# Score tiles by parity and half: 416 keys instead of 512 in the dilated attention of a hybrid block

## The chip, the cores and the metric

The kernel runs on one core of one Trainium2 chip. The metric is the device time of one execution in microseconds (us): the median of three runs for the kernel before and, later, for the changed one. A profile is of one further execution, with its own time and with the span from its first to its last instruction.

## What is computed

One encoder layer over 512 tokens of width 2048. Two mixers read the same projection; the change touches the first, attention with 16 heads of 64. Three dilated patterns share one softmax, so a query sees a key if any pattern allows the distance:

```python
for window, dilation in ((128, 1), (512, 4), (2048, 16)):
    o_p, lse_p = dilated_window_attention(aq, ak, av, rel_bias, window, dilation)
    # keys at 0, +-dilation, ... +-window/2
mix_w = jax.nn.softmax(jnp.stack(lses, axis=0), axis=0)
att = jnp.einsum('pbsh,pbshe->bshe', mix_w, jnp.stack(outs, axis=0))
```

Odd distances are allowed by the first pattern alone, up to 64; the others have even distances only. The rest of the layer (adaLN, the gated linear attention GLA, gates, output projection, norms) stays as it is.

## The kernel before

TensorE's matmuls take fp32 data as a rounded high part and a low part: `three` (lines 221 to 223) adds high x high, high x low and low x high. The kernel goes through the layer in stages: conditioning and the first products (tiles `sta`, `stb`), then units of projection products (`qk2`, `qk4`, `qk6`, `gk`, then values, gates, output). A unit has 8 groups of weights, 64 ticks of three 512-column products each, and a list of side work with places between 0 and 1 that `unit` puts between the ticks. The order of TensorE is this written order; DVE, ACT, POOL and SP get theirs from the tile framework. SP's queue issues nearly all loads and the copies from SBUF to SBUF, in order.

The attention is side work of the four units `qk2` to `gk`, four heads each. A head has four score tiles of 128 queries by 512 keys:

- `qk_evict` (lines 736 to 748) takes queries (reversed) and keys of two heads from PSUM. `qs` holds the high part in one half of the partitions and the low part in the other; `ks` and `kl` hold the keys' high and low part in both halves, the second copy by DMA.
- `score` multiplies `qs` with `ks` and with `kl` (lines 787, 788), adds the bias from `g` and finds the row's extreme on DVE (791), exponentiates on ACT (794), scales on POOL (801). `g` is a table of biases shifted by a column per partition, so that a slice of it fits a tile of reversed queries; it is loaded from `grow` in DRAM.
- `turn`, two tiles later, transposes four blocks of 128 x 128 (line 813) and writes high and low parts of the turned block `pt` (817 on ACT, 818 on DVE). `pt` covers two tiles, 256 queries; the pool has room for two such blocks.
- `values`, three tiles after the second of its two score tiles, multiplies `pt` with the values `vv` (line 827, eight matmuls) and adds up into `cat` (830, 834).

The items' places come from `ATT_AT`: start 0.17, span 0.8, and shifts of the first two and the last. Weights come through four `raw` buffers; `fetch` asks for them two groups ahead. Small sums for other stages (`S`, `rawv`) run on DVE beside the scores.

Of the kernel before, what the change touches and what calls it, by code (L numbers as in the profile page):

```python
# [79 lines left out]
def _runs():  # L80
# [6 lines left out]
    for j in range(2):  # L87
        cols = np.arange(512 * j, min(512 * j + 512, NREL))
        part = []
        for b, v in enumerate(seen):  # L90
            c = cols[bucket[cols] == v] - 512 * j
            if len(c):
                assert len(c) == c[-1] + 1 - c[0]
                if len(c) == 1 and part and part[-1][3]:
# [15 lines left out]
ATT_AT = (0.17, 0.8, 0.04, 0.05, 0.05)  # L110
# [72 lines left out]
def block_kernel(ctx: ExitStack, tc: tile.TileContext, a: dict):  # L183
# [6 lines left out]
    t2 = mid.enter_context(tc.tile_pool(name="t2", bufs=16))  # L190
# [144 lines left out]
    def row_part(j, i):  # L335
# [4 lines left out]
        for lo, hi, b, single in RUNS[j][i]:  # L340
            if single:
                tt(t[:, lo:hi], t[:, lo:hi], rel[:, b:b + hi - lo], op=ALU.subtract)
# [192 lines left out]
    def sum_col():  # L535
        psb["col"] = PJ("psc")
        for i in range(4):
            mm(psb["col"][:, i:i + 1], ssum[:, i * P:i * P + P], ones[:, 0:1], start=True, stop=True)
# [25 lines left out]
    def first_products(z, e):  # L564
# [3 lines left out]
        for i in range(4):  # L568
            j, t = 4 * z + i, slice(P * i, P * i + P)
# [4 lines left out]
    def products(st, k, j):  # L574
# [3 lines left out]
        if st == "a":  # L578
            t, c = slice(j % 4 * P, j % 4 * P + P), slice(j // 4 * 512, j // 4 * 512 + 512)
# [85 lines left out]
    for z in range(4):  # L665
        task(("row", z), "ACT", 0.9, [("uh", 7 + z), "rowl"], 50, lambda z=z: row_part(z // 2, z % 2))
# [60 lines left out]

    def qk_evict(p, psq, psk):
# [3 lines left out]
        for j in range(2):  # L732
            own = slice(64 * j, 64 * j + 64)
            oth = slice(64 - 64 * j, 128 - 64 * j)
            qs = T2(f"qs{p}{j}", F32R)
            act(qs[own], psq[own, ::-1], AF.Copy, scale=-0.125)
            stt(qs[oth], psq[own, ::-1], -0.125, qs[own].bitcast(F32),
                op0=ALU.mult, op1=ALU.subtract)
            stacks[2 * p + j] = [qs, None, None, own]
        for j in range(2):  # L740
            own = slice(64 * j, 64 * j + 64)
            oth = slice(64 - 64 * j, 128 - 64 * j)
            ks = T2(f"ks{p}{j}", F32R)
            kl = T2(f"kl{p}{j}", F32R)
            act(ks[own], psk[own], AF.Copy)
            nc.sync.dma_start(ks[oth].bitcast(F32), ks[own].bitcast(F32))
            tt(kl[own], psk[own], ks[own].bitcast(F32), op=ALU.subtract)
            nc.sync.dma_start(kl[oth].bitcast(F32), kl[own].bitcast(F32))
            stacks[2 * p + j][1:3] = ks, kl
# [16 lines left out]

    def attention(pairs):

        tiles = [(2 * p + j, i) for p in pairs for j in range(2) for i in range(4)]
        gt, pt, pr_ = {}, {}, {}  # L770
        heads = [2 * p + j for p in pairs for j in range(2)]

        def g_load(h):
            g = gp.tile([P, 896], F32, tag="g", name=f"g{h}")
            nc.sync.dma_start(g, bass.AP(grow.tensor, grow.offset + h * 1024, [[1, P], [1, 896]]))
            gt[h] = g

        def score(h, i):
            def go():
# [4 lines left out]
                qs, ks, kl, _ = stacks[h]  # L784
                q = slice(P * i, P * i + P)
# [920 lines left out]
```

## Time and profile before

| what | value |
|---|---|
| median of three runs | 919.68 us (919.38 to 919.89) |
| time of the profiled execution | 919.28 us |
| its span | 917.5 us |
| granted TensorE clock, mean | 0.996 of full |
| the attention's part of the span | about 190 to 455 us |
| one unit of it (qk4, from its first transposition to that of qk6) | 66.3 us |
| score tiles, turned tiles, value groups | 64, 64, 32 |
| bytes moved by DMA | 238.13 MB, 260 GB/s in the mean |

A line of the costliest groups has the source line, the engine, the operation, output and input tiles with shapes and the count, then busy us and mean ns of one, then the engine's idle time before them and what ended it. Matmuls are pipelined: the busy time of one overlaps the next, and what one costs is read from the distance of the starts.

### The profile page before, as it was taken

To read this page: it belongs to the slowest core of one execution; us is meant where nothing else is said; L and a number is where in the kernel's file an instruction comes from. 1 tells how busy PE (TensorE), PEld (TensorE's weight loads), DVE (VectorE), ACT (ScalarE), POOL (GpSimd) and SP (SyncE) were. 2 spreads that over 40 slices of the span, in tenths; PEclk is the share of its full clock that TensorE was granted. 3 is DMA by queue.
4 is the path that set the end of the run, shared out by engine and by line. 5 is a ranking of instruction groups with operands and counts; after the bars stand their busy time and mean duration, and the time that the engine had idled before them with its cause. 6 is when DMAs were issued, how large, how long until landed. Compare 5 with 4: busy or idle time off the path is not lost.

```text
span 917.5 us, 12263 instructions
## 1 busy us (share of the span) xinstructions
PE 902.5 (98%) x4327; PEld 749.9 (82%) x4327; DVE 715.8 (78%) x1043; ACT 490.7 (53%) x790; POOL 113.4 (12%) x168
## 2 busy tenths in 40 slices
PE   8999999999999999999999999999999999999996
PEld 6888888888888888888878788888888888888884
DVE  8988799877778878877659668586686649798786
ACT  5553533565555655655657554363654238455464
POOL 0000000012323223222100101111120100000001
PEclk9999999999999999999999999999999999999998
DMA  9999498567789898886778869877787887877863
GB/s 350 406 413 398 165 358 321 185 190 208 215 233 282 246 251 252 246 238 207 218 241 261 283 212 278 261 206 237 213 289 212 265 276 264 291 294 241 303 224 149
DMA packets 61671, 238.13 MB, mean 260 GB/s; under 512 B 8133, under 2 KB 8421, under 8 KB 52265
## 3 DMA queue, kind: packets, MB, share of 16 engines
q1 hardware_dynamic: 54850, 195.03, 59.6%
q0 software_dynamic: 6464, 42.01, 20.0%
q8 instruction: 34, 0.56, 0.2%
q10 hardware_dynamic: 296, 0.30, 0.1%
q14 instruction: 27, 0.22, 0.1%
HBM read 224.64 MB, written 50.42 MB: 300 GB/s over the span
## 4 chain that ended last, share of the span: by engine, by line
PE 90%; DVE 4%; DMA 2%; ACT 2%; issue 1%; SPq 0%; DVEq 0%; ACTq 0%
PE ps_qk L221 5%; PE ps_qk L222 5%; PE ps_qk L223 5%; PE g L223 4%; PE g L222 4%; PE g L221 4%; PE o L827 3%; PE stb L223 3%; PE stb L222 3%; PE stb L221 3%; PE t L813 3%; PE ps_ag L221 3%; PE ps_ag L223 3%; PE ps_ag L222 3%; PE sta L222 3%; PE sta L223 3%
## 5 line engine op out<-in xcount | busy, mean ns | idle before, releaser
L794 ACT ACTIVATE p<-p,st 128x512 f32<-128x512 f32 x64 | 46.2, 723 | 55.0 <-DVE st L791 54.6
L320 DVE CUSTOM_DVE_ANT_0 cb<-cb,sb,c_bcond 128x2048 f32<-128x2048 f32 (+1 forms) x32 | 73.5, 2297 | 0.3 <-DMA cb<-in_wm 0.2
L801 POOL TENSOR_SCALAR p<-p,st 128x512 f32<-128x512 f32 x62 | 47.7, 770 | 185.1 <-DVE st L797 135.8
L791 DVE CUSTOM_DVE_ANT_0 p<-s,g 128x512 f32<-128x512 f32 x64 | 43.8, 686 | 16.4 <-PE s L788 14.1
L818 DVE TENSOR_TENSOR pt<-t,pt 128x512 fp32r<-128x512 f32 x64 | 43.8, 688 | 12.0 <-ACT pt L817 11.5
L817 ACT ACTIVATE pt<-t 128x512 fp32r<-128x512 f32 x64 | 37.9, 592 | 11.7 <-PE t L813 10.9
L421 POOL DMA_DIRECT2D T<-in_w_o x32 | 23.2, 724 | 165.7 <-ACT V2h L485 13.7
L813 PEld LDWEIGHTS t<-c_ident,p 128*128 128x128 f32 x256 | 31.4, 140 | 9.7 <-POOL p L801 1.3
L813 PE MATMUL t<-c_ident,p 128*128 128x128 f32 x256 | 38.5, 273 | 0.1
L827 PEld LDWEIGHTS o<-pt,vv 128*128 128x128 f32 x256 | 34.7, 188 | 2.9
L827 PE MATMUL o<-pt,vv 128*128 128x256 f32 x256 | 35.5, 281 | 0.0
L787 PE MATMUL s<-ks,qs 128*128 128x512 f32 x64 | 25.1, 392 | 0.0
L788 PE MATMUL s<-kl,qs 128*128 128x512 f32 x64 | 25.0, 390 | 0.0
L1000 ACT ACTIVATE sq<-st,sc 128x256 f32<-128x256 f32 x24 | 12.2, 508 | 19.3 <-DVE st L990 11.3
L320 DVE CUSTOM_DVE_ANT_0 rawg<-rawg,crow,c_bcond 128x1024 f32<-128x1024 f32 x16 | 20.3, 1280 | 2.0 <-DMA rawg<-in_wg 2.0
L320 DVE CUSTOM_DVE_ANT_0 rawg<-rawg,crow,gate 128x1024 f32<-128x1024 f32 x16 | 20.4, 1280 | 0.8 <-DMA rawg<-in_wg 0.8
L1479 POOL TENSOR_SCALAR x<-x,rn 128x512 f32<-128x512 f32 x2 | 2.3, 1164 | 147.8 <-ACT rn L1468 143.3
L421 POOL DMA_DIRECT2D T3V<-in_w_gv x8 | 5.6, 695 | 119.8 <-ACT qk21h L485 119.8
L830 ACT ACTIVATE oh<-o 64x256 f32<-64x256 f32 x32 | 12.2, 382 | 12.8 <-PE o L827 12.2
L834 DVE TENSOR_TENSOR cat<-o,oh 64x256 f32<-64x256 f32 x32 | 13.3, 417 | 7.1 <-ACT oh L830 6.7
L549 ACT ACTIVATE h_hi<-xt,shift 128x512 fp32r<-128x512 f32 x16 | 11.5, 720 | 13.0 <-DVE shift L320 13.0
L421 POOL DMA_DIRECT2D T<-T x16 | 8.4, 527 | 80.5 <-ACT V18h L485 9.7
(1653 smaller groups left out, 3066.2 us busy)
## 6 DMA issues: line engine op xcount, KB each, us to landing
cb<-in_wm SPq DMA_DIRECT2D x31, 1024.0 KB, 8.6
T<-in_w_o POOLq DMA_DIRECT2D x32, 512.0 KB, 6.3
rawg<-in_wg SPq DMA_DIRECT2D x32, 512.0 KB, 5.6
raw_O<-in_w_o SPq DMA_DIRECT2D x32, 512.0 KB, 4.7
raw_qk<-in_w_qk SPq DMA_DIRECT2D x24, 512.0 KB, 4.2
raw_O<-T SPq DMA_DIRECT2D x24, 512.0 KB, 5.4
rawb<-in_w_sb SPq DMA_DIRECT2D x16, 512.0 KB, 5.8
rawv<-in_wv SPq DMA_DIRECT2D x16, 512.0 KB, 4.7
```

The lines of the kernel that those rows point to most:

```text
L221: mm(ps, lh, rh, start=first, stop=False, skip_group_check=more)
L222: mm(ps, ll, rh, start=False, stop=False, skip_group_check=more)
L223: mm(ps, lh, rl, start=False, stop=last, skip_group_check=more)
L320: return nc.vector.tensor_tensor_reduce(out=w, in0=w, in1=with_, op0=ALU.mult, op1=ALU.add, scale=1.0, scalar=init, accum_out=dst)
L421: move = nc.gpsimd.dma_start(dst, src, max_dma_last_dim=8192, **how).ins
L791: top = nc.vector.tensor_tensor_reduce(out=t, in0=ps, in1=gt[h][:, P * i:P * i + 512], op0=ALU.add, op1=ALU.min, scale=1.0, scalar=3e38, a ...
L794: act(t, t, AF.Exp, bias=st[:, 0:1], scale=-1.0, accum_out=st[:, 1:2])
L801: last["pool"] = nc.gpsimd.tensor_scalar(t, t, st[:, 2:3], 1.0, op0=ALU.mult, op1=ALU.mult).ins
L813: nc.tensor.transpose(pk[:, kt * P:kt * P + P], t[:, kt * P:kt * P + P], ident)
L817: act(hi, src, AF.Copy)
L818: tt(lo, src, hi.bitcast(F32), op=ALU.subtract)
L827: mm(po[:, :256], vv[h // 4][:, kt, h % 4, :], t[:, w, kt, :], start=kt == 0 and w == 0, stop=kt == 3 and w == 1)
```

## The change

Tokens are put in the order of parity and half (`TOKENS`): even tokens of the first half, of the second, odd ones of the first, of the second. A score tile then holds one parity of one half of the queries (128 of them), and of the keys all 256 of its own parity and the 160 of the other parity that lie within 64: 416 columns.

- The key tile holds high parts in one half of the partitions and low parts in the other, with even, odd and again even keys (768 columns; the last 256 by DMA), so that each tile's 416 keys are one slice. Both parts of the queries are now laid in both halves, by DMA. Queries and keys are read from PSUM with every second column.
- The bias row is stored by parity and `g` loaded in four pieces; two of the four tiles of a head add their bias in two pieces.
- Of a tile three blocks of 128 keys are transposed into the block `pt` of its query parity. The remaining 32 keys of both halves are transposed, copied to a tile `r` and laid into `pt` by two DMAs (`rest`). The other three quarters of those two blocks are zero; they are set once, and there are two `pt` in all.
- `values` runs five tiles after instead of three, ahead of the turn that writes the same block next, and takes the blocks with the remainders third and last.
- For space the GLA's queries go to DRAM before the attention and are loaded again after it; some small GLA tiles move to another pool.

```diff
-ATT_AT = (0.17, 0.8, 0.04, 0.05, 0.05)
+ATT_AT = (0.17, 0.8, 0.04, 0.05, 0.02, 0.1)
+NK = 416
+KEYS_AT = (96, 256, 352, 0)
+G_PIECES = ((96, 160, 0), (512, 384, 160), (128, 161, 544), (97, 160, 705))
+BIAS_AT = (((0, 416, 0),), ((0, 416, 288),),
+           ((0, 160, 705), (160, 416, 160)), ((0, 256, 288), (256, 416, 545)))
+CHUNK_OF = ((1, 2, 3, 0), (3, 0, 1, 2))
+TOKENS = [slice(256 * c + a, 256 * c + 256, 2) for a in range(2) for c in range(2)]
...
-    t2 = mid.enter_context(tc.tile_pool(name="t2", bufs=16))
+    t2 = mid.enter_context(tc.tile_pool(name="t2", bufs=15))
...
-            t, c = slice(j % 4 * P, j % 4 * P + P), slice(j // 4 * 512, j // 4 * 512 + 512)
+            t, c = TOKENS[j % 4], slice(j // 4 * 512, j // 4 * 512 + 512)
...
+    def by_parity(t, parts):
+        return t[parts, :512].rearrange("p (a c) -> p a c", a=2)
+    def key_tile(h):
+        q = h % 4
+        if q == 0:
+            return two.tile([P, 1024], F32R, tag="l", name=f"ks{h}")
+        if q == 3:
+            return kp.tile([P, 768], F32R, tag="ks", name=f"ks{h}")
+        if h // 4 not in key_pair:
+            key_pair[h // 4] = B8(f"ks{h}", [2, 768], F32R)
+        return key_pair[h // 4][:, q - 1, :]
...
-            qs = T2(f"qs{p}{j}", F32R)
-            act(qs[own], psq[own, ::-1], AF.Copy, scale=-0.125)
-            stt(qs[oth], psq[own, ::-1], -0.125, qs[own].bitcast(F32),
+            qh, ql = T2(f"qh{p}{j}", F32R), T2(f"ql{p}{j}", F32R)
+            src = psq[own, ::-1].rearrange("p (c e) -> p e c", e=2)
+            act(by_parity(qh, own), src, AF.Copy, scale=-0.125)
+            nc.sync.dma_start(qh[oth].bitcast(F32), qh[own].bitcast(F32))
+            stt(by_parity(ql, own), src, -0.125, by_parity(qh.bitcast(F32), own),
                 op0=ALU.mult, op1=ALU.subtract)
+            nc.sync.dma_start(ql[oth].bitcast(F32), ql[own].bitcast(F32))
...
-            act(ks[own], psk[own], AF.Copy)
-            nc.sync.dma_start(ks[oth].bitcast(F32), ks[own].bitcast(F32))
-            tt(kl[own], psk[own], ks[own].bitcast(F32), op=ALU.subtract)
-            nc.sync.dma_start(kl[oth].bitcast(F32), kl[own].bitcast(F32))
+            ks = key_tile(2 * p + j)
+            src = psk[own].rearrange("p (c a) -> p a c", a=2)
+            act(by_parity(ks, own), src, AF.Copy)
+            tt(by_parity(ks, oth), src, by_parity(ks.bitcast(F32), own), op=ALU.subtract)
+            nc.sync.dma_start(ks[:, 512:768].bitcast(F32), ks[:, 0:256].bitcast(F32))
...
-                mm(ps, qs[:, q], ks, start=True, stop=False)
-                mm(ps, qs[:, q], kl, start=False, stop=True)
+                k = slice(KEYS_AT[i], KEYS_AT[i] + NK)
+                mm(ps[:, :NK], qh[:, q], ks[:, k], start=True, stop=False)
+                mm(ps[:, :NK], ql[:, q], ks[:, k], start=False, stop=True)
...
+                for z, (lo, hi, at) in enumerate(BIAS_AT[i]):
+                    to = st[:, 0:1] if hi == NK else st[:, 3:4]
+                    top = nc.vector.tensor_tensor_reduce(
+                        out=t[:, lo:hi], in0=ps[:, lo:hi], in1=gt[h][:, at:at + hi - lo], op0=ALU.add, op1=ALU.min,
+                        scale=1.0, scalar=least, accum_out=to).ins
+                    least = to
...
+                e, half = divmod(i, 2)
+                if len(pts) == e:
+                    pts.append(B8(f"pt{e}", [2, 4, 256], F32R))
+                    nc.gpsimd.memset(pts[e][:, :, 3, 0:P].bitcast(F32), 0.0)
+                    nc.gpsimd.memset(pts[e][:, :, 0, P:2 * P].bitcast(F32), 0.0)
...
-                for kt in range(4):
-                    nc.tensor.transpose(pk[:, kt * P:kt * P + P], t[:, kt * P:kt * P + P], ident)
+                for kt in range(3):
+                    nc.tensor.transpose(pk[:, kt * P:kt * P + P], t[:, first_ + kt * P:first_ + kt * P + P], ident)
...
+        def rest(h, e):
+            pk = PJ(f"r{h}{e}")
+            for half, c in ((0, 0), (1, 384)):
+                nc.tensor.transpose(pk[:32, half * P:half * P + P], pr_.pop((h, 2 * e + half))[:, c:c + 32], ident)
+            st = T2(f"r{h}{e}", F32R, 32)
+            act(st[:, :256], pk[:32, :256], AF.Copy)
+            tt(st[:, 256:], pk[:32, :256], st[:, :256].bitcast(F32), op=ALU.subtract)
+            st4 = st.bitcast(F32).rearrange("p (w half q) -> p w half q", w=2, half=2)
+            for half, rows, c in ((0, slice(96, 128), 3), (1, slice(0, 32), 0)):
+                nc.sync.dma_start(pts[e][rows, :, c, P * half:P * half + P].bitcast(F32), st4[:, :, half, :])
...
+                order = (1, 2, 3, 0)
+                for n_, c in enumerate(order):
                     for w in range(2):
+                        mm(po[:, :256], vv[h // 4][:, CHUNK_OF[e][c], h % 4, :], t[:, w, c, :],
+                           start=n_ == 0 and w == 0, stop=n_ == 3 and w == 1)
...
-        for x in range(n + 4):
+        for x in range(n + 5):
             if x < n:
                 items.append(score(*tiles[x]))
+            v = x - 5
+            if 0 <= v < n and v % 2 == 1:
+                items.append(values(tiles[v][0], tiles[v][1] // 2))
             if 2 <= x <= n + 1:
                 items.append(turn(*tiles[x - 2]))
-            if x == n:
-                continue
-            for v in (x - 4, x - 3) if x == n + 1 else (x - 3,):
-                if 0 <= v < n and tiles[v][1] % 2 == 1:
-                    items.append(values(tiles[v][0], tiles[v][1] // 2))
...
+        at[-2] += move_next
         at[-1] += move_last
...
+    gq_rows = dp.tile([P, 2048], F32, tag="gq_rows", name="gq_rows")
+    nc.sync.dma_start(gq_rows, gla["q"].rearrange("p k c -> p (k c)"))
+    def gq_load():
+        gla["q"] = B8("gqr", [4, 512])
+        nc.sync.dma_start(gla["q"].rearrange("p k c -> p (k c)"), gq_rows)
...
-    values_unit([(0.03, up_load), (0.2, up_split), (0.235, lr_stack), (0.93, lambda: cond_half(0))] + gla_head(0))
+    values_unit([(0.02, gq_load), (0.03, up_load), (0.2, up_split), (0.235, lr_stack), (0.93, lambda: cond_half(0))] + gla_head(0))
```

The order of the engines shows what moves at the two places that matter below. On TensorE, before, at the second tile of a half head in unit `qk4` (`t` the turned tile, `ps_qk` the projection, `o` the value product of the half head just turned, shapes of the outputs; in brackets whose semaphores a row waits for):

```order
L813 MATMUL t_2413<-c_ident,p_2338 128x128 [waits DVE_49,Pool_49]
L813 MATMUL t_2413<-c_ident,p_2338 128x128 x3
L221 MATMUL ps_qk_2_2227<-h_hi,qk42h 128x512
L222 MATMUL ps_qk_2_2227<-h_hi,qk42l 128x512
L223 MATMUL ps_qk_2_2227<-h_lo,qk42h 128x512
L827 MATMUL o_2423<-pt_2351,vv_1097 128x256 [waits DVE_49]
L827 MATMUL o_2423<-pt_2351,vv_1097 128x256 x7
```

And now, toward the end of unit `qk2` (`r` the remainders of both tiles, 32 rows each; `o_2208` belongs to the half head before):

```order
L865 MATMUL r_2192<-c_ident,p_2050 32x128
L865 MATMUL r_2192<-c_ident,p_2091 32x128
L229 MATMUL ps_qk_0_1573<-h_hi,qk27h 128x512
L230 MATMUL ps_qk_0_1573<-h_hi,qk27l 128x512
L231 MATMUL ps_qk_0_1573<-h_lo,qk27h 128x512
L880 MATMUL o_2208<-pt_1745,vv_990 128x256 [waits DVE_49]
L880 MATMUL o_2208<-pt_1745,vv_990 128x256 x3
L880 MATMUL o_2208<-pt_1745,vv_990 128x256 [waits DMAHW3_49]
L880 MATMUL o_2208<-pt_1745,vv_990 128x256
L880 MATMUL o_2208<-pt_1745,vv_990 128x256 [waits DMAHW4_49]
L880 MATMUL o_2208<-pt_1745,vv_990 128x256
```

The value product has two more waits, each for a DMA, and it belongs to an earlier half head. On SP's queue before, in the middle of unit `qk2` (`raw_qk` weights, `g` the bias table, `S` a store of small sums):

```order
L368 DMA raw_qk_2232<-in_w_qk 128x1024 [waits DMAHW2_49,DVE_49]
L775 DMA g_2223<-grow 128x896 [waits DMAHW3_49,DVE_49]
L1129 DMA S_1502<-S_1923 128x512 [waits DMAHW4_49,DVE_49]
L368 DMA raw_qk_2283<-in_w_qk 128x1024 [waits DMAHW5_49,DVE_49]
L1129 DMA S_1496<-S_1998 128x512 [waits DMAHW6_49,DVE_49]
L775 DMA g_2307<-grow 128x896 [waits DMAHW7_49,DVE_49]
L902 DMA rawv_2295<-in_wv 128x1024 [waits DMAHW0_49,DVE_49]
```

The same stretch now:

```order
L871 DMA pt_1677<-r_1871 32x2x128 [waits DMAHW4_49,DVE_49]
L871 DMA pt_1677<-r_1871 32x2x128 [waits DMAHW5_49,PE_49]
L376 DMA raw_qk_2203<-in_w_qk 128x1024 [waits DMAHW6_49,DVE_49]
L1181 DMA S_1514<-S_1854 128x512 [waits DMAHW7_49,DVE_49]
L871 DMA pt_1745<-r_1954 32x2x128 [waits DMAHW0_49,DVE_49]
L871 DMA pt_1745<-r_1954 32x2x128 [waits DMAHW1_49,PE_49]
L376 DMA raw_qk_2326<-in_w_qk 128x1024 [waits DMAHW2_49,DVE_49]
L804 DMA g_2314<-grow 128x160 [waits DMAHW3_49,DVE_49]
L1181 DMA S_1516<-S_1973 128x512 [waits DMAHW4_49,DVE_49]
L804 DMA g_2314<-grow 128x384 [waits DMAHW5_49]
L804 DMA g_2314<-grow 128x161 [waits DMAHW6_49]
L804 DMA g_2314<-grow 128x160 [waits DMAHW7_49]
```

The remainders' copies stand among the weights, and the bias table takes four rows instead of one; each row also waits for the DMA eight rows ahead (the numbers of DMAHW go round from 0 to 7).

More of the change, by code (lines that the diff above doesn't have):

```diff
@@ L822, in go, with values @@
+        def values(h, e):
             def go():
-                t = pt.pop((h, half))
-                po = PA(f"o{h}{half}")
-                for kt in range(4):
+                t = pts[e]
+                po = PA(f"o{h}{e}")
+                order = (1, 2, 3, 0)
+                for n_, c in enumerate(order):
                     for w in range(2):
-                        mm(po[:, :256], vv[h // 4][:, kt, h % 4, :], t[:, w, kt, :],
-                           start=kt == 0 and w == 0, stop=kt == 3 and w == 1)
@@ L1644, in _constants @@
     row = np.zeros(1024, f)
[L1645 removed]
+    bias = np.where(mult > 0, -np.log(np.maximum(mult, 1)), BIG)
+    row[:512], row[512:NREL] = bias[0::2], bias[1::2]
     j, i = np.arange(P)[:, None], np.arange(P)[None, :]
```

74 lines of the change are left out of this document (38 added, 36 removed).

## The prediction, made before the changed kernel ran

> **What bounds the kernel now.** I read the page's busy shares first, then the chain of waits, then the busy time of two whole projection units (columns: length, then busy us and count of PE, PEld, DVE, ACT and POOL, granted clock, DMA share, GB/s).
>
> ```profile
> span 917.5 us, 12263 instructions
> PE 902.5 (98%) x4327; PEld 749.9 (82%) x4327; DVE 715.8 (78%) x1043; ACT 490.7 (53%) x790; POOL 113.4 (12%) x168
> PE 90%; DVE 4%; DMA 2%; ACT 2%; issue 1%; SPq 0%; DVEq 0%; ACTq 0%
> 266.64:332.96 66.32, 66.30 (x354) 55.78 (x353) 53.74 (x110) 37.58 (x72) 19.02 (x26) 1.00 0.91 269
> 332.96:399.29 66.33, 66.31 (x355) 55.81 (x353) 53.47 (x112) 37.69 (x72) 19.51 (x27) 1.00 0.85 246
> ```
>
> The change lies in the attention, which is woven into four such units between about 190 and 455 us. There TensorE has 0.02 us of idle in 66. DVE is busy for 81% of it, ACT for 57%, the DMA engines for 85 to 91%. So what TensorE is spared comes off the time, any wait of TensorE is added whole, and the other engines count only where they make it wait.
>
> **The score products.** A busy time of one matmul overlaps its neighbours, so I go by starts in the timeline (start, duration, engine, line, tiles).
>
> ```profile
> 206.42 1.11 PE L827 MATMUL o<-pt,vv 128*128 128x256 f32 x8
> 207.37 0.40 PE L221 MATMUL ps_qk<-h_hi,qk22h 128*128 128x512 f32 x1
> 207.84 0.39 PE L223 MATMUL ps_qk<-h_lo,qk22h 128*128 128x512 f32 x1
> ...
> 209.67 0.39 PE L223 MATMUL ps_qk<-h_lo,qk23h 128*128 128x512 f32 x1
> 209.90 0.60 PE L813 MATMUL t<-c_ident,p 128*128 128x128 f32 x4
> 210.25 0.48 PE L221 MATMUL ps_qk<-h_hi,qk23h 128*128 128x512 f32 x1
> 210.57 0.40 PE L222 MATMUL ps_qk<-h_hi,qk23l 128*128 128x512 f32 x1
> ```
>
> Eight 512-column matmuls lie between 207.84 and 209.67 (six of L221 to L223, two scores): 0.229 us each. Eight 256-column ones take 206.42 to 207.37: 0.119. The slope is 0.43 ns a column, so 416 columns cost 0.188, which is 0.041 less; with 128 score matmuls, **5.3 us** (5.5 if it goes in proportion). I take 5.4.
>
> **The transpositions.** Four took 210.57 - 209.90 less one 512-column matmul: 0.44, or 0.11 each. Each tile had four; now it has three and one that gives 32 rows: 192 + 64 = 256, as before. What does a 32-row one cost? The nearest rows are products that fill 64 output rows, against the score's 128:
>
> ```profile
> L787 PE MATMUL s<-ks,qs 128*128 128x512 f32 x64 | 25.1, 392 | 0.0
> L1210 PE MATMUL plr<-h_hi,lrs 128*64 128x512 f32 x16 | 6.2, 389 | 0.0
> ```
>
> Half the rows, the same time: the streamed columns set it, and those are the 128 of the identity in either case. I take a gain of 0; the other end is a quarter of the price, 64 x 0.083 = 5.3 us of gain. The value products stay at eight per half head.
>
> **ACT, DVE and POOL.** Mean ns of one, from the costliest groups:
>
> ```profile
> L794 ACT ACTIVATE p<-p,st 128x512 f32<-128x512 f32 x64 | 46.2, 723 | 55.0 <-DVE st L791 54.6
> L791 DVE CUSTOM_DVE_ANT_0 p<-s,g 128x512 f32<-128x512 f32 x64 | 43.8, 686 | 16.4 <-PE s L788 14.1
> L818 DVE TENSOR_TENSOR pt<-t,pt 128x512 fp32r<-128x512 f32 x64 | 43.8, 688 | 12.0 <-ACT pt L817 11.5
> L817 ACT ACTIVATE pt<-t 128x512 fp32r<-128x512 f32 x64 | 37.9, 592 | 11.7 <-PE t L813 10.9
> L830 ACT ACTIVATE oh<-o 64x256 f32<-64x256 f32 x32 | 12.2, 382 | 12.8 <-PE o L827 12.2
> L834 DVE TENSOR_TENSOR cat<-o,oh 64x256 f32<-64x256 f32 x32 | 13.3, 417 | 7.1 <-ACT oh L830 6.7
> ```
>
> DVE goes at (688 - 417)/256 = 1.06 ns a column. Per head: two bias steps of 416 columns (584 each, 2 x 102 less), two in pieces of 160 and 256 (317 + 417, 2 x 48 more, and two more accumulator reads of about 83), four low parts of 384 (4 x 136 less), two new ones of 256 (2 x 417): 0.35 us more. ACT at 0.82 a column: 4 x (79 + 105) less, 2 x 382 more: nothing. With four heads to a unit DVE goes from 54 to 55 of 66 us; TensorE's work covers it, and without that cover it would be 5.6 us in all. POOL's scaling (62 of 0.77 us each) only gets shorter.
>
> **The wait that is added.** The 32-column remainders of two tiles are transposed, copied and rounded (lines L867, L868 of the changed kernel), and then two copies on SP's queue carry them to other partitions of the turned block. The value product waits for both. Before, it waited for DVE alone. The chain, first as it is, in the timeline, then the queue's cost and landing of the copies most like the new ones, within 183 to 460 us (ns min/median/max; us to landing of ks, of kl):
>
> ```profile
> 205.29 0.60 PE L813 MATMUL t<-c_ident,p 128*128 128x128 f32 x4
> 206.62 0.58 ACT L817 ACTIVATE pt<-t 128x512 fp32r<-128x512 f32 x1
> 207.23 0.69 DVE L818 TENSOR_TENSOR pt<-t,pt 128x512 fp32r<-128x512 f32 x1 [0.32 <-ACT pt L817]
> ...
> L746 SPq DMA_DIRECT2D ks<-ks x16: 461/464/619, 188.5 to 390.8; - x16
> DMA to landing us min/median/max: 2.2/5.4/8.6
> DMA to landing us min/median/max: 2.2/5.2/8.0
> ```
>
> From the end of the transpositions (205.89) to DVE's end (207.92) are 2.03 us. Now 0.14 less for three blocks, 0.22 less because the two small transpositions come behind, 0.42 more for the remainder on DVE (its ACT copy runs beside DVE), 0.46 for the first copy in SP's queue: 2.55, plus landing. What stands ahead of these copies on SP (bias rows, weights) or of the remainder on DVE is not counted.
>
> TensorE's cover is read from the changed order and the prices above. The value products take the block with the remainder of the first tile third and that of the second last. For r_2192, in the piece of TensorE's order that stands ahead of this text, TensorE has before the waiting product 18 products of 512 columns (4.12), the eight value products of the half head before and four of its own (1.43) and eight transpositions (0.88): 6.4 us. The same count over the 32 half heads gives 6.4 (4 of them, the last but one of each unit), 7.6 (4), 8.0 (4), 8.5 (4), 8.9 (4) and 9.6 (12). So a copy may land after 3.9, 5.0, 5.4, 6.0, 6.4 or 7.0 us; the second copy is issued 0.46 later and needed 0.24 later, which I leave out. Landing at 2.2: nobody waits. At the median, 5.3: 4 x 1.4 + 4 x 0.3 = 6.8 us. At 8.6: 4 x (4.7 + 3.6 + 3.2 + 2.6 + 2.2) + 12 x 1.6 = 84. Weighting these a quarter, a half and a quarter gives 24.4. But each cover holds the value products of the half head before, and their wait lengthens it, so about half is paid: **12 us**. Both ends stay for the range: 0 and 42.
>
> Behind a waiting value product stands all of TensorE's further work, the projection's too, so nothing makes up for it. The weights behind the copies on SP's queue have four buffers and are asked for two groups of products ahead; they have that to lose first.
>
> [...]
>
> **The rest.** Copies of both query parts replace those of both key parts, one for one; the keys' wrap and the remainders add 4 x 256 KB to a unit that moves 269 GB/s x 66.3 us = 17.8 MB, 6% more, and no weight is late now, so 0, or some 1 us if the 0.91 share fills up. The GLA's queries go out to DRAM and come back, 1 MB each way; the load is issued at 0.02 and used at 0.3 of the values unit, over 20 us later, and the nearest loads of that size land in 8.6:
>
> ```profile
> cb<-in_wm SPq DMA_DIRECT2D x31, 1024.0 KB, 8.6
> ```
>
> The bias row's shorter pieces fall into the first stage, before the attention, on ACT (14 more of at most 104 columns). The parity order of the tokens changes weight loads alone there, each beside a 0.229 us matmul: 0.
>
> **Sum.** The profiled execution took 919.28 us (span 917.5 and 1.8 around it); the median is 0.40 above it. 919.28 - 5.4 + 12.2 = 926.1, with the 0.4: **926.5**.
>
> **Rivals.**
> *The copies land in time* (the other side). Place: the first copy-fed value product; price: only the 5.4 us gained: 914.3. It decides where landing stays under 3.9 us throughout. For it: the minimum of 2.2, and copies of 32 KB instead of 128 KB. Against it: weights of 512 KB stand right ahead in the same queue.
> *The slow end everywhere.* In the changed order each SP row waits for the semaphore of the row eight ahead; with 130 rows more in the queue (399 before, 529 now), copies are issued late and land near 8 us: 914.3 + 42 = 956. For it: landing already reaches 8.6 in the bunches at a unit's end. Against: only there.
> *Strided reads of PSUM.* Queries and keys are now read from PSUM with every second column. No row shows that; reversed, L736 costs what forward L745 does:
>
> ```profile
> L745 ACT ACTIVATE ks<-ps_qk 64x512 fp32r<-64x512 f32 x12 | 7.1, 594 | 3.9 <-DVE kl L747 3.6
> L736 ACT ACTIVATE qs<-ps_qk 64x512 fp32r<-64x512 f32 x12 | 7.1, 590 | 0.2
> 322.13 0.69 DVE L737 SCALAR_TENSOR_TENSOR qs<-ps_qk,qs 64x512 fp32r<-64x512 f32 x1
> ...
> 324.64 0.39 PE L221 MATMUL ps_qk<-h_hi,qk60h 128*128 128x512 f32 x1
> ```
>
> If each costs double, DVE's eight reads at a unit's end take 8 x 0.69 = 5.5 us more; the third bank is free at 322.82 and written at 324.64, a slack of 1.8, so three boundaries lose 3.7 each: 914.3 + 11 = 925.4 by itself. [...]
>
> **How the numbers follow.** The forecast has 0.47, landing in time 0.32, the slow end 0.13, strided reads 0.08. A measurement of this kernel can tell about 0.2%, 1.8 us, from no change. Of the forecast's share I put 0.04 on faster and 0.08 on within 0.2%, since the wait may come to about 5 us. Faster: 0.32 + 0.04 = 0.36; same 0.08; slower 0.35 + 0.13 + 0.08 = 0.56. The forecast's own range is 916 to 936; the 8-in-10 range goes from landing in time and a microsecond of the transpositions' other end, 913, to three quarters of the way to the slow end, 945.
>
> **What would show it.** Right: score matmuls 0.188 us apart at start; TensorE idle, or a late start, right ahead of the third value matmul of a half head, released by a DMA, some 12 us in all, most of it near unit ends; no idle elsewhere. Wrong, if the value groups still take 0.95 us (in time), if the small transpositions take 0.03 instead of 0.11, if L761 to L773 of the changed kernel take over 1 us, or if TensorE waits at the scores for copies of queries or keys, which I took to be covered.

## The result: slower by 6.6%, and the profile after

| what | before | after |
|---|---|---|
| median of the runs, beside each other | 919.53 us (918.37 to 919.89) | 980.69 us (976.69 to 982.46) |
| ratio, with its 95% interval | | 1.0661 (1.0623 to 1.07) |
| span of the profiled execution | 917.5 us | 980.6 us |
| granted TensorE clock, mean | 0.996 | 0.977 |

The direction was foreseen, the size was not: 61 us where 7 were predicted. The page of the changed kernel, the head, the busy share of TensorE, the chain of waits and the two groups with the longest idle time:

```profile
span 980.6 us, 12703 instructions
PE 918.0 (94%) x4327; PEld 762.7 (78%) x4327; DVE 717.3 (73%) x1139; ACT 488.8 (50%) x836; POOL 109.2 (11%) x172
...
PE 75%; DMA 13%; DVE 5%; ACT 3%; issue 2%; SPq 0%; DVEq 0%; POOL 0%; ACTq 0%; POOLq 0%
...
L880 PE MATMUL o<-pt,vv 128*128 128x256 f32 x256 | 43.0, 302 | 47.9 <-DMA pt<-r 47.8
L880 PEld LDWEIGHTS o<-pt,vv 128*128 128x128 f32 x256 | 37.9, 199 | 54.4 <-DMA pt<-r 51.6
```

TensorE now stands idle for 47.9 us ahead of the value products, and 47.8 of it end with the landing of a copy `pt<-r`. Before, the same group had none (from 183 to 520 us):

```profile
L827 PE MATMUL o<-pt,vv 128*128 128x256 f32 x256 | 35.5, 281 | 0.0
```

DMA, 2% of the chain before, has 13%. The second thing to see is that TensorE is busy for 918.0 us, 15.5 more than before, though its matmuls have become shorter. The stretches of the attention in the changed kernel (us, then busy us and count of PE, PEld, DVE, ACT and POOL, granted clock, DMA share, GB/s) show why:

```profile
183.00:260.00 77.00, 70.01 (x355) 58.24 (x354) 50.13 (x125) 38.65 (x82) 17.58 (x31) 0.98 0.78 204
260.00:330.00 70.00, 57.50 (x282) 48.33 (x281) 43.64 (x107) 29.83 (x66) 12.69 (x19) 0.90 0.77 206
330.00:400.00 70.00, 56.77 (x286) 47.81 (x285) 44.43 (x109) 30.00 (x67) 14.03 (x22) 0.93 0.79 210
400.00:480.00 80.00, 64.86 (x321) 54.21 (x321) 47.50 (x121) 32.48 (x72) 16.50 (x23) 0.91 0.74 210
```

The granted clock falls with the idle time. One long wait, in the timeline of TensorE (start, duration, engine, line, tiles; in brackets the idle time before and what ended it):

```profile
261.81 0.63 PE L880 MATMUL o<-pt,vv 128*128 128x256 f32 x4
269.61 1.23 PE L880 MATMUL o<-pt,vv 128*128 128x256 f32 x4 [7.17 <-DMA pt<-r]
270.63 0.63 PE L229 MATMUL ps_qk<-h_hi,qk27h 128*128 128x512 f32 x1
271.06 0.63 PE L230 MATMUL ps_qk<-h_hi,qk27l 128*128 128x512 f32 x1
...
273.73 0.39 PE L231 MATMUL ps_qk<-h_lo,qk40h 128*128 128x512 f32 x1
273.96 0.40 PE L229 MATMUL ps_qk<-h_hi,qk40h 128*128 128x512 f32 x1
```

Four value products run, the fifth waits 7.17 us for a copy, and the 512-column products after it start 0.43 us apart instead of 0.23 until 273.4. The stretches around it:

```profile
258.00:262.00 4.00, 4.00 (x24) 3.31 (x23) 2.72 (x6) 2.49 (x7) 0.00 (x0) 1.00 0.95 211
...
264.00:266.00 2.00, 0.00 (x0) 0.00 (x0) 0.62 (x1) 0.00 (x0) 0.00 (x0) 1.00 1.04 256
266.00:268.00 2.00, 0.00 (x0) 0.00 (x0) 0.00 (x0) 0.00 (x0) 0.00 (x0) 0.63 0.92 259
268.00:270.00 2.00, 0.39 (x2) 0.39 (x3) 0.00 (x0) 0.00 (x0) 0.00 (x0) 0.50 0.55 156
270.00:273.00 3.00, 3.00 (x10) 2.52 (x10) 1.11 (x2) 0.97 (x2) 0.00 (x0) 0.50 0.68 185
```

The copy is issued at 256.88 us and has landed at 269.57, after 12.7 us. Until 268 us the 16 DMA engines are busy nearly all the time (0.92 to 1.04; a packet counts where it starts, so a stretch can pass 1), and TensorE comes back at half its clock. In the trace's clock record the attention has seven stretches at 0.50, 41.0 us long in sum, and TensorE works in 27.5 us of them, which costs half of that, 13.8 us. (The four stretches of the attention above give the same 41: twice 0.02 x 77 + 0.10 x 70 + 0.07 x 70 + 0.09 x 80.)

Where the time went, by idle time and clock record: 917.5 - 5.4 (shorter scores) + 48.8 (50.6 us of idle against 1.8 before) + 13.8 (half clock) + 1.9 (first stage, below) = 976.6. The 4.0 us left are about what 22 interruptions cost when the first matmul after each takes 0.39 us alone instead of 0.23 in the stream: 22 x 0.16 = 3.5, an estimate from these rows.

How late are the copies? DMA issues of the changed kernel between 183 and 520 us (count, KB each, median us to landing), with the share of POOL's queue:

```profile
q0 software_dynamic: 3136, 20.58, 24.5%
...
qh<-qh SPq DMA_DIRECT2D x16, 128.0 KB, 5.5
ql<-ql SPq DMA_DIRECT2D x16, 128.0 KB, 2.5
ks<-ks SPq DMA_DIRECT2D x16, 128.0 KB, 2.0
pt<-r SPq DMA_DIRECT2D x64, 32.0 KB, 7.3
```

A copy of 32 KB lands after 7.3 us, at most 12.7, while a copy of 128 KB on the same queue, `ks`, takes 2.0. So it isn't its size. Two things may set it apart: weights and bias rows stand ahead of it on SP's queue, and it runs all through a unit, beside POOL's block sums (sums of weight blocks in DRAM, its queue is q0); most copies of keys are issued just after TensorE's long wait at a unit's end, when the DMA engines have run low (above, a share of 0.55 from 268 us on).

### The profile page after: what moved, and what is told of

Same layout as the page of the kernel before. It is cut to its first block, busy times and chain, and to the rows that moved or that the text cites. A ratio compares the mean times of both kernels' runs of the same rounds, so it can differ in the third digit from the quotient of the medians.

```text
span 980.6 us, 12703 instructions
## 1 busy us (share of the span) xinstructions
PE 918.0 (94%) x4327; PEld 762.7 (78%) x4327; DVE 717.3 (73%) x1139; ACT 488.8 (50%) x836; POOL 109.2 (11%) x172
## 4 chain that ended last, share of the span: by engine, by line
PE 75%; DMA 13%; DVE 5%; ACT 3%; issue 2%; SPq 0%; DVEq 0%; POOL 0%; ACTq 0%; POOLq 0%
DMA pt<-r 11%; PE g L231 4%; PE g L230 3%; PE g L229 3%; PE stb L231 3%; PE stb L229 3%; PE stb L230 3%; PE sta L230 3%; PE sta L229 3%; PE sta L231 3%; PE ps_ag L229 3%; PE ps_ag L231 3%; PE ps_ag L230 3%; PE o L880 2%; PE ps_qk L229 2%; PE ps_qk L230 2%
## 5 line engine op out<-in xcount | busy, mean ns | idle before, releaser
L880 PE MATMUL o<-pt,vv 128*128 128x256 f32 x256 | 43.0, 302 | 47.9 <-DMA pt<-r 47.8
L836 POOL TENSOR_SCALAR p<-p,st 128x416 f32<-128x416 f32 x62 | 42.5, 686 | 248.4 <-DVE st L832 157.0
L829 ACT ACTIVATE p<-p,st 128x416 f32<-128x416 f32 x64 | 40.9, 639 | 54.0 <-DVE st L825 44.6
L825 DVE CUSTOM_DVE_ANT_0 p<-s,g 128x416 f32<-128x416 f32 (+1 forms) x64 | 30.6, 478 | 26.4 <-PE s L818 20.0
L856 DVE TENSOR_TENSOR pt<-t,pt 128x384 fp32r<-128x384 f32 x64 | 35.4, 553 | 16.4 <-ACT pt L855 16.2
L855 ACT ACTIVATE pt<-t 128x384 fp32r<-128x384 f32 x64 | 31.0, 485 | 24.2 <-PE t L851 23.8
L851 PE MATMUL t<-c_ident,p 128*128 128x128 f32 x192 | 32.5, 280 | 0.0
L817 PE MATMUL s<-ks,qh 128*128 128x416 f32 x64 | 22.7, 355 | 1.0 <-DMA ks<-ks 1.0
L818 PE MATMUL s<-ks,ql 128*128 128x416 f32 x64 | 22.8, 356 | 0.2 <-DMA ql<-ql 0.2
L832 DVE RECIPROCAL st<-st 128x1 f32<-128x1 f32 x64 | 10.0, 156 | 12.4 <-ACT p L829 12.3
```

Of the source, the lines that this page charges most:

```text
L825: top = nc.vector.tensor_tensor_reduce(out=t[:, lo:hi], in0=ps[:, lo:hi], in1=gt[h][:, at:at + hi - lo], op0=ALU.add, op1=ALU.min, scale=1 ...
L829: act(t, t, AF.Exp, bias=st[:, 0:1], scale=-1.0, accum_out=st[:, 1:2])
L836: last["pool"] = nc.gpsimd.tensor_scalar(t, t, st[:, 2:3], 1.0, op0=ALU.mult, op1=ALU.mult).ins
L851: nc.tensor.transpose(pk[:, kt * P:kt * P + P], t[:, first_ + kt * P:first_ + kt * P + P], ident)
L855: act(hi, src, AF.Copy)
L856: tt(lo, src, hi.bitcast(F32), op=ALU.subtract)
```

## The experiments

All ratios are against the kernel before on the same chip.

| kernel | median us | ratio (95% interval) | idle us | at half clock, us |
|---|---|---|---|---|
| the change | 980.69 | 1.0661 (1.0623 to 1.07) | 50.6 | 41.0 |
| no_copies | 924.65 | 1.0061 (1.0046 to 1.0076) | 7.1 | 3.4 |
| no_wait | 923.63 | 1.0045 (1.003 to 1.0059) | 7.4 | 0 |
| act_queue | 984.93 | 1.0703 (1.0677 to 1.0729) | 45.4 | 44.4 |
| padded | 928.67 | 1.0099 (1.0081 to 1.0116) | 9.7 | 3.4 |
| after_short | 973.78 | 1.0594 (1.0576 to 1.0612) | 39.2 | 37.5 |
| before_short | 919.44 | 1.0001 (0.9992 to 1.001) | 0.3 | 0 |
| padded_short | 926.23 | 1.0077 (1.0062 to 1.0092) | 8.4 | 0 |
| padded_short_late | 923.62 | 1.0052 (1.0037 to 1.0067) | 4.4 | 6.8 |
| no_sums | 930.09 | 1.0118 (1.0098 to 1.0138) | 10.9 | 0 |
| no_sums_act | 937.87 | 1.0207 (1.0164 to 1.025) | 15.6 | 3.4 |
| plain_tokens | 921.32 | 1.0024 (1.0015 to 1.0033) | 5.1 | 6.8 |
| padded_shift | 923.81 | 1.0045 (1.0032 to 1.0057) | 6.7 | 6.8 |
| padded_row | 917.53 | 0.9981 (0.9972 to 0.999) | 1.8 | 0 |

Idle is TensorE's from 183 us to 12 us before the end; half clock is the length of the stretches at 0.50 there. The kernel before has 1.8 and 0.

### Is it the wait for the copies?

**no_copies** leaves the two copies out:

```diff
-            for half, rows, c in ((0, slice(96, 128), 3), (1, slice(0, 32), 0)):
-                nc.sync.dma_start(pts[e][rows, :, c, P * half:P * half + P].bitcast(F32), st4[:, :, half, :])
```

> Leaves out the two copies of the remainders, so the value products read zeros for the 32 remaining keys of each tile; every other instruction stays. Theory A (the wait for the copies is the whole loss: 48 us of idle TensorE ahead of L880, and a clock of 0.90 to 0.93 in the units as its consequence): 913 to 917 us, no idle ahead of L880, clock above 0.99 in all units. Rival B (something else of the change, the bias in pieces, the copies of queries, the order of DVE, costs it): over 940 us, and the idle moves to another line.

**no_wait** keeps them, with another destination:

```diff
-                nc.sync.dma_start(pts[e][rows, :, c, P * half:P * half + P].bitcast(F32), st4[:, :, half, :])
+                aside = dp.tile([32, 2, P], F32, tag=f"aside{h}{e}{half}", name=f"as{h}{e}{half}")
+                nc.sync.dma_start(aside, st4[:, :, half, :])
```

> Keeps all 64 copies in their places in SP's queue with the same bytes, but sends them to scratch rows in DRAM, so nothing waits for them; the value products read zeros for the 32 remaining keys. Theory A (only the wait costs): as without the copies, 913 to 918 us, though the copies still take about 7 us to land. Rival C (the 64 copies crowd the queue: weights and bias rows behind them come late, whoever waits for the copies): over 935 us, with TensorE waiting for weights.

They came out 56 and 57 us under the change. The DMA issues of no_wait, between 183 and 520 us:

```profile
as<-r SPq DMA_DIRECT2D x64, 32.0 KB, 7.2
```

The copies are there and as late as ever, 7.2 us, and cost nothing. So the loss is the wait and its consequence, not the traffic, and theory C fell. But both kernels stand 4 to 5 us above the kernel before, where 5.4 less was due, and neither came under 918. Theory A was right for 56 us; the 9.5 to 10.5 us above that sum it does not explain. What is left is seen in the groups of no_wait on TensorE from 183 to 520 us:

```profile
L851 PE MATMUL t<-c_ident,p 128*128 128x128 f32 x192 | 31.5, 273 | 1.6 <-POOL p L836 1.6
L817 PE MATMUL s<-ks,qh 128*128 128x416 f32 x64 | 23.0, 359 | 5.4 <-DMA qh<-qh 2.2 <-DVE st L825 1.6 <-DMA ks<-ks 1.1
```

With the big wait gone, the first scores of a unit wait for copies of queries and keys. In the changed kernel these waits come to 1.2 us only; that the long waits there hid the rest is likely, and not shown.

### Why are the copies late: queue, packets or load?

**act_queue** takes them out of SP's queue:

```diff
-                nc.sync.dma_start(pts[e][rows, :, c, P * half:P * half + P].bitcast(F32), st4[:, :, half, :])
+                nc.scalar.dma_start(pts[e][rows, :, c, P * half:P * half + P].bitcast(F32), st4[:, :, half, :])
```

> The two copies are issued from ACT's queue instead of SP's; all else as in the change. Theory A1 (they land late because they stand behind weights and bias rows in SP's queue): median landing from 7.3 down to 2 to 4 us, idle ahead of L880 under 15 us, 918 to 935 us. Rival A2 (they land late because the 16 DMA engines are shared, whatever the queue): landing still near 7 us, 965 to 985 us. ACT pays 64 issues, at most 0.6 us each, beside TensorE's work.

DMA issues and TensorE's group in act_queue:

```profile
pt<-r ACTq DMA_DIRECT2D x64, 32.0 KB, 6.4
```

```profile
L880 PE MATMUL o<-pt,vv 128*128 128x256 f32 x248 | 44.5, 306 | 43.3 <-DMA pt<-r 43.1
```

On a queue of their own the copies land after 6.4 us instead of 7.3, and TensorE waits 43.3 us, in 22 waits of at most 5.2 instead of 15 of at most 8.9. The time is no better, 984.93: the half clock costs more (TensorE works for 39.1 us in it, where it was 27.5). These are A2's numbers. The place in the queue, my first theory, was not it: 984.93 us on ACT's queue against 980.69 on SP's.

**after_short** cuts POOL's sums into smaller rows, and **before_short** does the same to the kernel before:

```diff
-            move = nc.gpsimd.dma_start(dst, src, max_dma_last_dim=8192, **how).ins
+            move = nc.gpsimd.dma_start(dst, src, max_dma_last_dim=2048, **how).ins
```

> The changed kernel with one edit: POOL's block sums move the same bytes in rows of 2 KB instead of 8 KB. Theory P (a copy of remainders is served packet by packet in turn with POOL's queue, and every 8 KB packet of that queue, 0.63 us each, holds it up; over the copies, landing grows 0.56 us for each such packet that its DMA engine serves meanwhile): median landing from 7.3 to under 4.5 us, idle ahead of L880 from 48 to under 15 us, granted clock of 0.97 or more in all units, 930 to 945 us. Rival Q (only the load on the 16 DMA engines counts, however cut): landing stays at 6 to 8 us, 970 to 985 us.

> Control: the kernel before with the same edit of POOL's rows. TensorE had no idle there, so there is nothing to gain: 917 to 921 us under either theory. If the shorter rows cost by themselves (four times the descriptors on POOL, sums that come late): over 922 us.

The DMA issues of after_short between 183 and 520 us, and its group on TensorE:

```profile
q0 software_dynamic: 8192, 20.97, 26.6%
...
pt<-r SPq DMA_DIRECT2D x64, 32.0 KB, 6.1
```

```profile
L880 PE MATMUL o<-pt,vv 128*128 128x256 f32 x256 | 43.6, 301 | 36.8 <-DMA pt<-r 36.3
```

POOL's packets are 2.6 times as many with nearly the same bytes, and landing falls from 7.3 to 6.1 us, the idle from 47.9 to 36.8. Landing and time lie within rival Q's bounds, the landing at their lower end, and far from theory P's: the length of the other queue's packets matters a little, 7 us of time, and is not the main cause. The control shows that the edit itself costs nothing.

**no_sums** takes the load away:

```diff
         if what in BLOCK_SUMS and pair == "V":
+            nc.sync.dma_start(t, block(pair, "11", g))
...
         def go():
+            if pair == "V":
+                return
```

> The changed kernel without POOL's 32 block sums for the value weights; the values unit loads plain blocks in their place, so its products are of other weights. The copies of remainders stay on SP's queue. Theory L (POOL's sums, which keep the DMA engines full, make the copies late): median landing from 7.3 to under 4 us, idle ahead of L880 from 48 to under 12 us, half-clock stretches (41 us in the changed kernel) under 10 us, 920 to 935 us. Rival O (the copies wait their turn in SP's queue behind weights and bias rows): landing stays over 6 us, idle over 35 us, over 960 us.

**no_sums_act** is the same with the copies on ACT's queue.

> As the one before, without the 32 block sums, and with the copies of remainders issued from ACT's queue. Theory L alone: within 5 us of the one before. If queue order counts beside the load: landing about 2 us, no idle ahead of L880, 915 to 922 us. If neither counts: idle over 35 us as with ACT's queue alone (43 us).

The DMA issues and the group in no_sums:

```profile
q0 software_dynamic: 961, 6.30, 7.5%
...
pt<-r SPq DMA_DIRECT2D x64, 32.0 KB, 3.7
```

```profile
L886 PE MATMUL o<-pt,vv 128*128 128x256 f32 x256 | 38.0, 285 | 10.3 <-DMA pt<-r 10.3
```

With POOL's share down from 24.5 to 7.5%, landing is halved to 3.7 us though weights and bias rows still stand ahead of the copies on SP's queue; the idle falls from 47.9 to 10.3 us, the half clock disappears, and the time is 930.09, all as theory L had it. The scores' waits are gone too (0.0 us; the copies of queries, `qh`, land after 2.3 us instead of 5.5). On ACT's queue nothing is gained over that: landing 3.9, idle 14.7 ahead of the value products, 937.87. That is 7.8 us more, where theory L alone allowed 5, and its runs lie as far apart as 933 and 946 us; why was not followed up. So the load of POOL's sums on the DMA engines is most of what makes the copies late, and the queue's order is not. That the sums add in DRAM, or only their bytes, was not separated.

### The same computation without copies

**padded** lets the transpositions put the remainders in place. A score tile of 416 keys stands in a 512-column buffer, at its end for one half and at its start for the other, and POOL clears the other 96 columns; four whole transpositions then fill the block.

```diff
-                t = tile_[:, :NK]
+                pad = 96 if i % 2 == 0 else 0
+                t = tile_[:, pad:pad + NK]
+                nc.gpsimd.memset(tile_[:, 0:96] if pad else tile_[:, NK:512], 0.0)
...
-                for kt in range(3):
-                    nc.tensor.transpose(pk[:, kt * P:kt * P + P], t[:, first_ + kt * P:first_ + kt * P + P], ident)
+                for kt in range(4):
+                    c = (kt + 1) % 4 if half else (kt - 1) % 4
+                    nc.tensor.transpose(pk[:, c * P:c * P + P], t[:, kt * P:kt * P + P], ident)
...
-                if half:
-                    rest(h, e)
```

> Computes the whole reference without any copy: each score tile keeps its 416 keys inside a 512-column buffer whose other 96 columns POOL clears, so that four 128-column transpositions put the remainder straight on its rows; eviction is 512 wide as before the change (592 ns on ACT, 688 on DVE). Theory A: 919.5 less the 5.4 us of narrower score products, 913 to 916 us, no idle ahead of the value products. Rival B (something else of the change costs it): over 940 us. If POOL's clearing comes late, idle ahead of the transpositions instead.

It is 52 us faster than the change and 9 slower than before, between the two theories' times. What remains is 5.6 us of idle at the scores, much as in no_wait (5.4), so that part has nothing to do with the remainders, and 2.9 us at the transpositions, most of it behind POOL. **padded_short** adds the 2 KB rows, **padded_short_late** also starts the attention of a unit later (`ATT_AT` 0.21 and 0.76 instead of 0.17 and 0.8):

> The version without copies of remainders, with POOL's rows of 2 KB. What is left there are 5.6 us of scores that wait for copies of queries and keys at a unit's start and 2.9 us of transpositions behind POOL. Theory P: those copies land earlier too, the scores' waits fall under 2 us, 921 to 925 us. Rival Q: no change, 926 to 930 us.

> As the one before, and the attention's pieces of a unit begin 0.04 of the unit (2.6 us) later, in 0.76 instead of 0.80 of it. If the scores' waits are only a matter of the first slot: no wait for copies left, 918 to 922 us. Rival: the closer spacing makes the transpositions wait for the softmax instead, over 924 us.

Padded_short came out within its rival's interval (no change) and a microsecond above theory P's: 3.7 us of idle at the scores, 3.5 at the transpositions, so the shorter rows are not shown to help here. The late version came between theory and rival, 2.6 us below padded_short. Most of what was left stood at one place: 2.35 us of wait for a score at the second unit's start, behind DVE, and 6.8 us of half clock after it.

**plain_tokens** tests a term that I had put at nothing, the strided weights of the first stage (tokens in steps of two). It goes back to contiguous columns:

```diff
-TOKENS = [slice(256 * c + a, 256 * c + 256, 2) for a in range(2) for c in range(2)]
+TOKENS = [slice(P * i, P * i + P) for i in range(4)]
```

> The late version without copies and with rows of 2 KB (923.6 us), but the first stage takes the tokens in plain order, so the weights of its value projection are loaded from contiguous columns; the value products then meet keys and values in different orders. Theory S (a strided weight load takes 193 instead of 188 ns and sets the pitch of the 384 products of that stage, 0.2335 instead of 0.2285 us): 1.9 us less, the attention's first projection starts at 188 instead of 190 us, 921 to 922.5 us. Rival (the stage is set by something else, such as the bias row's pieces): no change.

The weight loads of two of that stage's groups (busy, mean ns), of the kernel before and of the changed one:

```profile
L221 PEld LDWEIGHTS sta<-sa7hi,h_hi 128*128 128x128 f32 x8 | 1.5, 188 | 0.3
```

```profile
L229 PEld LDWEIGHTS sta<-sa7hi,h_hi 128*128 128x128 f32 x8 | 1.5, 193 | 0.3
```

It came out at 921.32, 2.3 us less than 923.62 and within theory S's range. A load with every second column takes 5 ns longer, 193 against 188, and the 384 products of the stage start a median of 0.233 us apart instead of 0.227, though each load lies beside a longer product (0.39 us). Counted at 5 ns for each product, that is 1.9 us.

**padded_shift** makes the row of shifts at 0.3 of its unit instead of 0.05, **padded_row** at 0.7 of the unit before:

```diff
-        ps = unit(n, False, attention((p, p + 1)) + ([(0.05, shift_row)] if p == 2 else []))
+        ps = unit(n, False, attention((p, p + 1)) + ([(0.7, shift_row)] if p == 0 else []))
```

> The late version without copies and with rows of 2 KB, and the row of shifts is made at 0.3 of its unit instead of 0.05. The longest wait left (2.4 us for a score behind DVE, and the half clock of 6.8 us that follows) stands at that unit's start. Theory: that wait and the half clock go, 918 to 921 us, within 0.2% of before or better. Rival: the wait stays, since it comes from the evictions of queries and keys and not from the row: 922 to 925 us.

The waits of padded_shift from 276 to 300 us (engine, line, releaser: us, times, longest):

```profile
POOL p L838 <- DVE st L834: 18.6, 5, 10.3
...
DVE rawv L945 <- DMA shb<-srow: 6.0, 1, 6.0
...
PE t L851 <- POOL p L838: 4.4, 1, 4.4
```

The stall has moved with the row: DVE waits 6.0 us for the row's broadcast (`shb`, 1 MB), the softmax behind it on DVE waits, POOL's scaling waits for that, and TensorE for POOL. One late transfer held up three engines in a row. The time is the rival's, 923.81, for a reason that neither had.

> The late version without copies and with rows of 2 KB, and the row of shifts is made at 0.7 of the unit before, 23 us earlier. In the version with that row at 0.3, DVE waited 6.05 us for the row's broadcast (1 MB) and all behind it waited too, up to TensorE's 4.45 us for POOL; at 0.05 the same wait stands at the unit's start. Theory: that is the last late transfer of the attention; without it no half clock and under 2.5 us of idle, 917 to 920 us. Rival: another transfer is late in its place, 922 us or more.

TensorE's groups of padded_row from 183 to 520 us and its second stretch:

```profile
L851 PE MATMUL t<-c_ident,p 128*128 128x128 f32 x256 | 38.4, 272 | 0.9 <-DVE pt L856 0.6 <-DVE cat L873 0.3
...
L817 PE MATMUL s<-ks,qh 128*128 128x416 f32 x64 | 22.6, 353 | 0.0
```

```profile
260.00:330.00 70.00, 69.98 (x374) 59.70 (x373) 55.41 (x129) 39.08 (x77) 20.19 (x40) 1.00 0.98 255
```

TensorE is full again, with no half clock and the idle of before (1.8 us). The whole computation takes 917.53 us, ratio 0.9981 (0.9972 to 0.999): 63 us less than the change and 1.7 us less than the kernel before, which is under 0.2%. By the terms, 917.5 - 5.4 + 1.9 = 914.0 was due for its span, and it is 915.5; the 1.5 us between are not accounted for. The later start and the row's new place were not tried in the kernel before, so the 1.7 us are not shown to come from the scores alone. If they do, the gain is small, and the change as it was spent it many times over.

## The prediction, point by point

**Scores: right.** In the timeline of the changed kernel the two score products of a tile and the next one start 0.19 us apart; behind them stand the small transpositions:

```profile
204.73 0.35 PE L817 MATMUL s<-ks,qh 128*128 128x416 f32 x1
204.92 0.35 PE L818 MATMUL s<-ks,ql 128*128 128x416 f32 x1
205.11 0.39 PE L229 MATMUL ps_qk<-h_hi,qk22h 128*128 128x512 f32 x1
...
205.81 0.49 PE L851 MATMUL t<-c_ident,p 128*128 128x128 f32 x3
206.13 0.38 PE L865 MATMUL r<-c_ident,p 128*32 128x128 f32 x2
206.27 0.48 PE L229 MATMUL ps_qk<-h_hi,qk22h 128*128 128x512 f32 x1
206.59 0.39 PE L230 MATMUL ps_qk<-h_hi,qk22l 128*128 128x512 f32 x1
```

**Transpositions: right.** From 205.81 to 206.59 lie five of them and one 512-column product: (0.78 - 0.23)/5 = 0.11 each, the small ones too. A transposition with a quarter of the rows costs the whole price.

**DVE, ACT, POOL hidden: right while TensorE is busy.** The prices fit (a bias step of 416 columns 586 ns against 584, a remainder's low part 404 against 417; a bias step in two pieces 797 to 801 against 734). The transfers that DVE waits for were not looked at, though, and the row of shifts stood among them.

**The added wait: the mechanism right, its size wrong by a factor of four.** This is the step that failed. TensorE waits at the value products, nearly always at the fifth of the eight (the first that reads a copied block), released by a copy: 47.9 us instead of 12. About half of it, 24.6 us, lies in three waits at unit ends (269.6, 355.5 and 438.3 us) rather than most of it; another 15.1 us lie in four waits some 28 us into a unit. Three terms were off.

First the landing, the largest: I took 2.2, 5.3 and 8.6 us from the copies of keys before, and the trace has 2.4, 7.3 and 12.7. With the last two in the prediction's own covers the sum is 42.8 us at the median (4 x (3.4 + 2.3 + 1.9 + 1.3 + 0.9) + 12 x 0.3) and 216 at the maximum, so 75 weighted, 38 halved. The covers lie between 3.9 and 7.0 us, so 2 us more of landing made 6.8 us of wait into 42.8. The choice of rows was not the trouble: in the kernel before, the bias table, which goes through the whole unit on the same queue, landed in the same 5.3 us.

```profile
g<-grow SPq DMA_DIRECT2D x14, 448.0 KB, 5.3
```

The runs show that POOL's sums make the copies late (no_sums, 3.7 us); why these copies land 2 us later than the larger transfers did beside the same sums before is open. Second the halving: 47.9 of 75 were paid, about two thirds, not half. Third the chain ahead of the landing: from the end of the small transpositions to the issue of the first copy the trace has a median of 2.9 us, and 2.55 - 0.46 = 2.1 was counted.

**What follows a wait: left out.** The prediction counted a microsecond of idle as a microsecond. Here 48.8 us of added idle drew 13.8 us of half clock and some 4 us of restarts behind them, more than the prediction's whole wait.

**The rest at 0: wrong in two small terms**, 1.9 us for the strided weights and the scores' waits for copies, 1.2 us in the change and 5.4 in no_wait, where they are no longer hidden.

**The rivals.** Landing in time (914.3) fell: the copies took 2.4 us at least and 7.3 in the median. With the copies gone, padded_row came within 3.2 us of that sum, 1.9 of them the strided weights. The slow end everywhere (956) was nearest, for another reason than the one given: landing is late throughout, but not for the length of the queue. Another queue brought no time, and the copies are not issued late: in the changed kernel SP issues the first copy of a half head a median of 0.05 us after DVE has written the low part, 2.7 at most. Strided reads of PSUM fell: the doubled price in its sum was an assumption that no run shows. The changed kernel's groups on ACT and on DVE:

```profile
L761 ACT ACTIVATE qh<-ps_qk 64x512 fp32r<-64x512 f32 x12 | 7.0, 588 | 1.3 <-DVE ql L763 1.1
```

```profile
L763 DVE SCALAR_TENSOR_TENSOR ql<-ps_qk,qh 64x512 fp32r<-64x512 f32 x12 | 8.2, 686 | 0.9 <-ACT qh L761 0.7
```

Every second column costs 588 and 686 ns; the reads before, without a stride, cost 590 (L736, in the prediction) and 689:

```profile
L737 DVE SCALAR_TENSOR_TENSOR qs<-ps_qk,qs 64x512 fp32r<-64x512 f32 x12 | 8.3, 689 | 0.4
```

The range ended at 945, and so did not reach the time. The slow end had 0.13; the row that spoke for it, DMA engines 85 to 91% busy, was in the prediction's first fence and was not made into a landing time.

## What to carry to other kernels

A transfer put into the path of a full TensorE costs what it takes to land at that moment, under the load that other queues put on the DMA engines then (here 7.3 us in the median beside POOL's sums, 3.7 without most of them). Where its cover is about as long as its landing, the sum is steep: here, by the prediction's covers, 2 us more made 7 us of wait into 43. Redo it with a longer landing before you trust it, and count the slower clock after each long wait (here 13.8 us for 48.8 us of added idle). If the layout can be had without the transfer (here by 96 cleared columns and whole transpositions), that wait goes as a whole; in padded_row nothing on TensorE waits for POOL's clearing. When the great wait is gone, read the trace again: the waits that it hid come out, and here the last one was a broadcast that had been in time before.

## What the runs showed of the hardware

**Half clock followed waits, also short ones, and fell on the work behind them.** In the changed kernel's clock record the seven stretches at 0.50 in the attention last 3.41 us (three of them), 6.83 (three) and 10.24 (one). The one at the wait of 7.17 us goes from 266.54 to 273.37 us, 3.8 us past the end of the wait at 269.61. After a wait of 2.71 us that ended at 217.28 it came from 218.75 to 222.17, with TensorE never idle in it. In no_copies three waits of 0.70, 0.16 and 0.71 us, ended at 398.83, 399.41 and 401.27, came just ahead of 3.4 us at half clock (stretches as above):

```profile
398.00:401.00 3.00, 1.71 (x6) 0.86 (x5) 0.99 (x3) 0.91 (x2) 0.00 (x0) 1.00 1.02 191
401.00:405.00 4.00, 3.73 (x10) 3.10 (x11) 2.97 (x8) 1.11 (x4) 1.92 (x2) 0.57 0.97 258
```

**A strided load of weights is not free** though a longer product (0.39 us) runs beside it: 193 ns in the changed kernel against 188 before, and the products of the stage start a median of 0.233 us apart against 0.227.

**The same copy on the same queue lands at twice the speed when another queue is quieter.** The 32 KB copies `pt` on SP's queue landed after a median of 7.3 us in the changed kernel, where POOL's queue took 24.5% of the DMA engines' time between 183 and 520 us, and after 3.7 us in no_sums, where it took 7.5%.
